# Half of the first layer's modulation tiles beside the latent projections, with two weight buffers; the last branch's sum on VectorE; the residual loaded into its accumulator

## The chip, the cores and the metric

One core of a Trainium2 chip runs the whole kernel. The metric is the device time of one execution in microseconds: the median of the kernel's runs is 2621.69 us, from 2621.12 to 2623.41 in three runs.

The engines go by their short names in the profile: PE is TensorE, PEld its weight load, DVE is VectorE, ACT is ScalarE, POOL is GpSimd, SP is the engine that issues all of this kernel's transfers.

## What is computed

The reference is a diffusion trunk of two layers (called 0 and 1 here, as in the code), over 512 latent and 128 context tokens of width 1024. Each layer is a mixer and an MLP:

```
mod  = silu(cond) @ w_mod + b_mod        # six vectors of 1024 per layer, for two conditionings
h    = rms_norm(x) * (1 + mod[1]) + mod[0]
cols = h @ w_in                          # GLA, MLA latents, differential attention, gates
y_a, y_b, y_c = gla(cols), mla(cols), diff_attention(cols)
m    = sum over b of sigmoid(h @ w_gate[b]) * (y_b @ w_o[b])
x    = x + mod[2] * (m @ w_out)
h    = rms_norm(x) * (1 + mod[4]) + mod[3]
x    = x + mod[5] * (relu(h @ w1)**2 @ w2)
```

The latent tokens are modulated by one conditioning, the context tokens by the other. So `mod` of both layers depends on the conditionings alone and may be computed at any time before its use: kinds 0 and 1 before a layer's first norm, kind 2 in the output projection, 3 and 4 in the second norm, 5 behind the MLP.

## The kernel before

**Layout.** Activations lie with features on the partitions and the 640 tokens along the free dimension, in halves of 256 and 384 columns (`HALVES`). Every operand of a matmul is a pair of a high and a low part, and each product is three matmuls (L104 to L106 in `mm3`): high by high, high by low, low by high.

**Weights.** `load_w` (L89) loads a block of 512 KB (256 KB for wo) on SP (L94), ScalarE casts the high part (L97), and VectorE subtracts for the low one (L99); while `pool_lo` is set, in the latent projections, POOL does that subtraction. The buffers are those of tag w (wraw 2, whi and wlo 3); while pool w2 is open, blocks alternate with a second set (xraw 1, xhi and xlo 3).

**Modulation.** `mod_tile` (L202) computes 128 of the 6 x 1024 outputs of one layer: a load of 512 KB (L206, tile modw, one buffer), and two multiply-and-sum operations on VectorE (L209, one for each conditioning; their throwaway output is mjunk, the sum goes to modv). After every fourth tile `mod_fin` (L233) adds the bias. The first 16 tiles of layer 0 come at the start of the kernel, twelve of them by TensorE (`mod_first`) and four in buffers of their own (tile sraw). The other 80 tiles, 32 of layer 0 (kinds 2 to 5) and 48 of layer 1, are handed out one by one by `mod_some` (L248), all of them behind the attention branches of layer 0: 8 + 4 + 4 in the three merges (`MERGE_MODS`), 8 in the output projection (`OUT_MODS`), 56 in the MLP, one after each block of w1 and w2. Layer 1 has none to do.

**The latent projections.** `mla_down` (L607) projects h to the query latent, the key-value latent and a small tail, token tile by token tile of 128, with three generators: two tiles of each are started, then each is drained. It stands at the beginning of a layer, behind the first norm. In layer 0 it runs from about 50 to 115 us.

**Merge.** `merge` (L1203) runs once per branch b. For each of eight blocks m of 128 features it projects the branch's output by wo (L94), multiplies by the gate into th (L1232, VectorE), sums into mg[m] (L1234, POOL; branches 1 and 2), and for branch 2 splits mg[m] into mh and ml (L137 on ScalarE, L138 on VectorE), the input of the output projection.

**Output projection.** `out_proj` (L1257) takes m by m: a block of wout, the residual as xin (L1270, one load for each half, three buffers), the matmuls, and the addition into the new accumulator xs[m] (L1247, `add_res`), then the sum of squares for the next norm (L267, sqacc). mg and xs share the eight buffers of tag x. The MLP (L1281) follows.

**Order.** The instructions of an engine are not issued in the order of the source: a planner arranges them at compile time by when their inputs are ready. The trace shows it: the first block of w1 is loaded ahead of the last blocks of wout. SP issues all loads in one queue, and one that waits for its buffer holds those behind it.

**Pools.** A pool's space is reused when it closes; `mj` holds modw, mjunk and condb (the conditioning spread over the partitions). Tiles of a pool opened over the space of another wait until that one's tiles were used for the last time.

Of the kernel before, what the change touches and what calls it, by code (L numbers as in the profile page):

```python
# [11 lines left out]
F32 = mybir.dt.float32  # L12
# [4 lines left out]
ALU = mybir.AluOpType  # L17
# [20 lines left out]

SCAN_PROJ = (1, 2)
GROUPS = ((0, 1), (2, 3, 4))  # L40
MERGE_MODS = ((1, 1, 1, 1, 1, 1, 1, 1), (0, 1, 0, 1, 0, 1, 0, 1), (1, 1, 1, 1, 0, 0, 0, 0))
OUT_MODS = (2, 2, 2, 2, 0, 0, 0, 0)
MERGE_AHEAD = 3

SKEW = (3, 6, 3)
# [1 line left out]
TAGS = {  # L47
    "wraw": ("w", 2), "whi": ("w", 3), "wlo": ("w", 3), "xraw": ("w2", 1), "xhi": ("w2", 3), "xlo": ("w2", 3), "hh": ("h", 8), "hl": ("h", 8),
    "sm_m": ("small", 4), "sm_b": ("small", 4), "sm_s0": ("small", 4), "sm_s1": ("small", 4), "sm_r": ("small", 4),
    "rowb": ("tab", 1), "tabmq": ("tab", 1), "tabmk": ("tab", 1), "lampr": ("tab", 1),  # L50
    "krn": ("tab", 1), "aan": ("tab", 1), "krg": ("tab", 1), "krc": ("tab", 1), "sskr": ("tab", 1),
    "nlam": ("tab", 1), "ghalf": ("tab", 1), "gsub": ("tab", 1), "gqk": ("tab", 1),
    "x": ("x", 8), "sqacc": ("nrm", 1), "sqt": ("nrm", 2), "nt": ("nrm", 3),
    "yb": ("yb", 2), "yc": ("dif", 4), "pd0": ("dif", 4), "pd1": ("dif", 2), "gth": ("gth", 3),
# [5 lines left out]
    "mla_sq": ("mla", 1), "mla_v": ("mla", 6), "mla_kn": ("mla", 9), "mla_qn": ("mla", 5),  # L60
    "mla_pp": ("mla", 2), "mla_qh": ("mla", 2), "mla_ql": ("mla", 2), "mla_kh": ("mla", 2), "mla_kl": ("mla", 2),
    "pt": ("att", 4), "mla_th": ("mla", 2), "mla_tl": ("mla", 2), "mla_tmp": ("mla", 1), "mla_tmp2": ("mla", 1),
    "rt1_32": ("tab", 1), "rt2_32": ("tab", 1), "rt1_64": ("dfr", 1), "rt2_64": ("dfr", 1),
# [5 lines left out]
    "xin": ("xin", 3), "mjunk": ("mj", 1), "condb": ("mj", 1), "modw": ("mj", 1), "mraw": ("st", 2), "sraw": ("st", 4), "maskf": ("st", 2), "mrow": ("st", 2), "uh": ("mlp", 8), "ul": ("mlp", 8), "relu": ("mlp", 3),  # L69
# [5 lines left out]
class Net:  # L75
# [531 lines left out]
    def mla_down(self, l, h):  # L607

        self.qdn = [self.S([128, 384], F32, "qdn") for t in range(5)]
        self.kvn = [self.S([128, 256], F32, "kvn") for t in range(5)]  # L610
        gens = [self.proj_tail(l, h), self.proj_nat(l, 2, h, self.kvn),
                self.proj_nat(l, 3, h, [q[:, 0:256] for q in self.qdn])]
        for g in gens:
            for _ in range(2):
                next(g)
        for g in gens:
            self.drain(g)

    def mla_latent(self, l):

# [582 lines left out]
    def merge(self, l, b, h):  # L1203

        nc = self.nc
        if b == 0:
            self.ys = {}
            self.drain(self.merge_in(0))
        ys = self.ys[b]
        nxt = self.merge_in(b + 1) if b < 2 else iter(())  # L1210
        outs = []
        if b == 0:
            self.mg = [self.S([128, T], F32, "x") for m in range(8)]
        mg = self.mg
        for m in range(8):
            t = mg[m] if b == 0 else self.S([128, T], F32, "th")
            if (b, m) in self.early:
                nc.sync.dma_start(t, self.gd[b][:, m])
            else:
                for p, (c0, c1) in zip(self.gates(l, b, m, h), HALVES):  # L1220
                    nc.scalar.activation(t[:, c0:c1], p[:, :c1 - c0], AF.Tanh, scale=0.5)
            wo = self.load_w(self.a["wo"][l, b, m], [128, 4, 128])
            ws = [(wo[0][:, k], wo[1][:, k]) for k in range(4)]
            if b == 2:
                mh = self.S([128, T], F32R, "mh")
                ml = self.S([128, T], F32R, "ml")
                outs.append((mh, ml))
            for i, (c0, c1) in enumerate(HALVES):
                n = c1 - c0
                p = self.P([128, 512], "g")  # L1230
                self.gemm(p[:, :n], ws, ys, c0, c1)
                nc.vector.scalar_tensor_tensor(t[:, c0:c1], t[:, c0:c1], 1.0, p[:, :n], op0=ALU.add, op1=ALU.mult)  # L1232
                if b:
                    nc.gpsimd.tensor_tensor(mg[m][:, c0:c1], mg[m][:, c0:c1], t[:, c0:c1], op=ALU.add)  # L1234
                if b == 2:
                    self.split(mg[m][:, c0:c1], n, mh[:, c0:c1], ml[:, c0:c1])
            if m >= MERGE_AHEAD:
                next(nxt, None)
            self.mod_some(MERGE_MODS[b][m])
        self.drain(nxt)  # L1240
        return outs

    def add_res(self, l, kind, m, half, p, src, dst, o=0):

        c0 = HALVES[half][0]
        for p0, p1, s in PARTS[half]:
            self.nc.vector.scalar_tensor_tensor(  # L1247
                dst[:, p0:p1], p[:, p0 - c0:p1 - c0], self.moda[l][:, kind * 8 + m, s:s + 1], src[:, p0 - o:p1 - o],
                op0=ALU.mult, op1=ALU.add)

    def order(self, head, tail):
# [5 lines left out]
    def out_proj(self, l, ms, xsrc):  # L1257
        self.stat_begin()
        xs = [self.S([128, T], F32, "x") for k in range(8)]
        wts = {}  # L1260
        self.norm_begin()
        for m, i in self.order(0, SKEW[0]):
            if (m, i) == (8 - SKEW[0], 1):
                self.norm(l, 1, xs, 0)
            if m not in wts:
                w = self.load_w(self.a["wout"][l, m], [128, 8, 128])
                wts[m] = [(w[0][:, k], w[1][:, k]) for k in range(8)]
            c0, c1 = HALVES[i]
            xin = self.S([128, 384], F32, "xin")
            self.nc.sync.dma_start(xin[:, :c1 - c0], xsrc(m)[:, c0:c1])  # L1270
            p = self.P([128, 512], "g")
            self.gemm(p[:, :c1 - c0], wts[m], ms, c0, c1)
            self.add_res(l, 2, m, i, p, xin, xs[m], c0)
            self.stat_add(xs[m], i)
            if i and l == 0:
                self.mod_some(OUT_MODS[m])
        self.norm(l, 1, xs, 1)
        return xs
# [65 lines left out]
    def run(self):  # L1344
        nc, tc, a = self.nc, self.tc, self.a
        self.pools, self.open, self.turn, self.pool_lo = {}, set(), 0, True
        with ExitStack() as top:
# [13 lines left out]
            nx.enter_context(self.pool("nrm", "st", "mj"))  # L1361
# [20 lines left out]
            for l in range(DEPTH):  # L1382
                for st in (nx, xp):
                    st.close()
                xp, nx, pm, w2 = self.layer(l, self.h, w2, pm)
            for st in (nx, xp, pm, w2):
                st.close()

    def layer(self, l, h, w2, ps):
        nc, tc, a = self.nc, self.tc, self.a  # L1390
        self.tables(l)
        self.ghalf = self.S([128, 1], F32, "ghalf")
        nc.vector.tensor_scalar(self.ghalf, self.vec[:, l, 16:17], 0.5, None, op0=ALU.mult)
# [7 lines left out]
        fl, lat, latT, mla = ExitStack(), ExitStack(), ExitStack(), ExitStack()  # L1401
        fl.enter_context(self.pool("gth"))
        latT.enter_context(self.pool("latT"))
        lat.enter_context(self.pool("lat"))
        self.fillq.append(self.gla_r(l, h, range(4)))
        self.fillq.append(self.gates_early(l, 0, h, range(8)))
        self.fillq.append(self.gates_early(l, 1, h, range(8)))
        self.fillq.append(self.gates_early(l, 2, h, range(8)))
        self.pool_lo = True
        self.mla_down(l, h)  # L1410
        self.pool_lo = False
        self.fill(4)
# [53 lines left out]

        pm = self.psum("pn")
        w2 = ExitStack()
        xp, mo, nrm, xin, mrg, mrb = (ExitStack() for _ in range(6))
        self.pending = [(l, i) for i in range(16, 48)] if l == 0 else []  # L1470
        if l + 1 < DEPTH:
            self.pending += [(l + 1, i) for i in range(48)]
        if self.pending:
# [11 lines left out]
        ms = self.merge(l, 2, h)  # L1485
        mrg.close()
        w2.enter_context(self.pool("w2", side="right"))
        xin.enter_context(self.pool("xin"))
        xs = self.out_proj(l, ms, (lambda m: a["x"][:, m]) if l == 0 else (lambda m: self.xs_dram[:, m]))
        xin.close()  # L1490
        mo.close()
        with self.pool("mlp"):
            self.mlp(l, xs, self.h, l + 1 == DEPTH)
# [147 lines left out]
```

## Time and profile before

| | |
|---|---|
| median of the runs | 2621.69 us (2621.12 to 2623.41) |
| the profiled execution | 2621.01 us, its span 2619.2 us |
| mean granted TensorE clock | 0.985 |
| DVE, ACT, POOL busy | 61%, 45%, 17% of the span |
| chain that ended last, by engine | PE 56%, DVE 7%, ACT 3% |
| the same by line, the first that is not PE's | DMA modw<-wmod 2% |
| tiles of modulation behind the attention branches | 80, their loads from 597.2 to 1267.2 us |

The profile is of one execution on the chip. Its span runs from the first instruction to the last; the profiled execution's own time is 1.8 us longer. A row of a windows view gives how long each engine was busy in a stretch; the times behind that are in the same order on every row. A row of a waits view says which operation stood, what came last of what it waited for, and the total, the number and the longest of these waits. A row of a timeline gives the start and the duration, and in brackets how long the engine stood before it and for what.

### The profile page before, as it was taken

What the parts mean: (1) busy time and instruction counts of PE and PEld (TensorE: products, weight loads), DVE (VectorE), ACT (ScalarE), POOL (GpSimd) and SP (SyncE); (2) the same over time, 40 slices, a digit from 0 to 9 for tenths busy, and PEclk for the clock granted to TensorE, in tenths of its full rate; (3) what the DMA queues carried; (4) which work ended last, traced back from release to release, by engine and by line L of the source; (5) the groups of instructions that cost most, each with busy time, mean ns of one, the idle gap of its engine ahead of it and who ended that gap; (6) DMA issues with size and microseconds to landing.
All of it is one profiled execution on the core that took longest, in us unless ns stands there. A gap on an engine that the chain in (4) does not pass through costs nothing.

```text
span 2619.2 us, 45102 instructions
## 1 busy us (share of the span) xinstructions
PE 2517.7 (96%) x17596; PEld 2433.6 (93%) x17596; DVE 1594.1 (61%) x3635; ACT 1189.1 (45%) x2323; POOL 446.5 (17%) x582
## 2 busy tenths in 40 slices
PE   6999999899998999999989999998999999999999
PEld 3988999898998999999989889998989999999999
DVE  7387666676676876666565776666764455333332
ACT  4477677556322332231334767775652334132230
POOL 2022242110041011020221222511001201010010
PEclk8999999999998999999999999999999999999999
DMA  6111112312655454444321111122225342222221
GB/s 256 41 47 69 50 57 69 93 63 74 228 183 182 138 161 153 153 146 145 121 79 41 56 62 65 41 70 94 80 94 190 104 131 88 74 73 76 78 73 49
DMA packets 109589, 265.03 MB, mean 101 GB/s; under 512 B 12288, under 2 KB 46336, under 8 KB 108608
## 3 DMA queue, kind: packets, MB, share of 16 engines
q1 hardware_dynamic: 109376, 262.15, 30.1%
q8 instruction: 139, 2.28, 0.4%
q14 instruction: 74, 0.61, 0.1%
HBM read 232.71 MB, written 29.39 MB: 100 GB/s over the span
## 4 chain that ended last, share of the span: by engine, by line
PE 56%; DVE 7%; ACT 3%; issue 2%; DMA 2%; POOL 1%; SPq 0%; DVEq 0%; POOLq 0%; ACTq 0%
PE g L104 15%; PE g L105 15%; PE g L106 15%; DMA modw<-wmod 2%; PE f L104 1%; PE go L504 1%; PE f L105 1%; PE f L106 1%; DVE mjunk L209 1%; PE y L1024 1%; DVE sm_m L752 1%; PE g L820 1%; DMA xraw<-wout 1%; DVE wlo L99 0%; PE g L1016 0%
## 5 line engine op out<-in xcount | busy, mean ns | idle before, releaser
L97 ACT CAST whi<-wraw 128x1024 fp32r<-128x1024 f32 (+2 forms) x236 | 220.0, 933 | 414.5 <-PE g L105 346.4
L99 DVE TENSOR_TENSOR wlo<-wraw,whi 128x1024 fp32r<-128x1024 f32 (+3 forms) x230 | 256.9, 1118 | 210.8 <-ACT whi L97 203.9
L104 PE MATMUL g<-hh,whi 128*128 128x256 f32 (+1 forms) x992 | 311.7, 314 | 5.8 <-DVE gla_t L603 4.2
L106 PE MATMUL g<-hh,wlo 128*128 128x256 f32 (+1 forms) x992 | 310.0, 313 | 2.1 <-DVE wlo L99 2.1
L105 PE MATMUL g<-hl,whi 128*128 128x256 f32 (+1 forms) x992 | 309.8, 312 | 0.0
L1298 POOL TENSOR_TENSOR relu<-relu 128x256 f32<-128x256 f32 (+1 forms) x128 | 113.4, 887 | 801.1 <-ACT uh L1297 798.9
L209 DVE CUSTOM_DVE_ANT_0 mjunk<-modw,condb 128x1024 bf16<-128x1024 f32 x160 | 197.8, 1236 | 60.7 <-DMA modw<-wmod 60.1
L97 ACT CAST xhi<-xraw 128x1024 fp32r<-128x1024 f32 (+1 forms) x80 | 83.7, 1046 | 280.7 <-PE g L105 258.0
L1247 DVE SCALAR_TENSOR_TENSOR x<-g,moda,x 128x256 f32<-128x256 f32 (+1 forms) x192 | 78.4, 435 | 198.7 <-PE g L106 198.7
L104 PEld LDWEIGHTS g<-hh,whi 128*128 128x128 f32 x992 | 189.3, 191 | 7.3 <-issue 4.6
L106 PEld LDWEIGHTS g<-hh,wlo 128*128 128x128 f32 x992 | 189.5, 191 | 2.3 <-DVE wlo L99 2.3
L105 PEld LDWEIGHTS g<-hl,whi 128*128 128x128 f32 x992 | 189.6, 191 | 0.0
L104 PE MATMUL g<-hh,xhi 128*128 128x384 f32 (+1 forms) x544 | 168.1, 309 | 0.0
L106 PE MATMUL g<-hh,xlo 128*128 128x384 f32 (+1 forms) x544 | 168.0, 309 | 0.0
L105 PE MATMUL g<-hl,xhi 128*128 128x384 f32 (+1 forms) x544 | 167.8, 308 | 0.0
L105 PE MATMUL g<-ul,whi 128*128 128x384 f32 (+1 forms) x512 | 158.0, 309 | 0.6 <-DVE ul L1299 0.6
L104 PE MATMUL g<-uh,xhi 128*128 128x384 f32 (+1 forms) x512 | 158.2, 309 | 0.0
L106 PE MATMUL g<-uh,xlo 128*128 128x384 f32 (+1 forms) x512 | 158.0, 309 | 0.0
L105 PE MATMUL g<-ul,xhi 128*128 128x384 f32 (+1 forms) x512 | 158.0, 309 | 0.0
L106 PE MATMUL g<-uh,wlo 128*128 128x384 f32 (+1 forms) x512 | 158.0, 309 | 0.0
L104 PE MATMUL g<-uh,whi 128*128 128x384 f32 (+1 forms) x512 | 157.9, 308 | 0.0
L1234 POOL TENSOR_TENSOR x<-x,th 128x256 f32<-128x256 f32 x64 | 78.3, 1230 | 464.4 <-DVE th L1232 452.6
(445 smaller groups left out, 7751.5 us busy)
## 6 DMA issues: line engine op xcount, KB each, us to landing
modw<-wmod SPq DMA_DIRECT2D x80, 512.0 KB, 3.5
wraw<-w SPq DMA_DIRECT2D x64, 512.0 KB, 3.6
xraw<-w SPq DMA_DIRECT2D x64, 512.0 KB, 3.5
wraw<-wfm SPq DMA_DIRECT2D x62, 512.0 KB, 3.5
wraw<-wn SPq DMA_DIRECT2D x36, 512.0 KB, 3.7
wraw<-wo SPq DMA_DIRECT2D x48, 256.0 KB, 3.1
yin<-yd SPq DMA_DIRECT2D x24, 320.0 KB, 3.6
gd<-gth SPq DMA_DIRECT2D x36, 192.0 KB, 1.9
```

The source lines that it names most:

```text
L97: nc.scalar.copy(hi, raw)
L99: eng.tensor_tensor(lo, raw, hi.bitcast(F32), op=ALU.subtract)
L104: mm(out, wh, xh, start=first, stop=False)
L105: mm(out, wh, xl, start=False, stop=False)
L106: mm(out, wl, xh, start=False, stop=last)
L209: nc.vector.tensor_tensor_reduce(out=junk, in0=w, in1=self.condb[:, s], scale=1.0, scalar=0.0, op0=ALU.mult, op1=ALU.add, accum_out=self.m ...
L504: nc.tensor.matmul(p[:, hd], km[:, hd, cs], qm[:, hd, cs])
L752: nc.vector.tensor_reduce(out=nm, in_=sc, axis=ax, op=ALU.max, negate=True)
L820: nc.tensor.transpose(p[:, i * 256 + j * 128:i * 256 + j * 128 + 128], pts[j][:, (k0 + i) * 128:(k0 + i) * 128 + 128], self.ident)
L1234: nc.gpsimd.tensor_tensor(mg[m][:, c0:c1], mg[m][:, c0:c1], t[:, c0:c1], op=ALU.add)
L1247: self.nc.vector.scalar_tensor_tensor(dst[:, p0:p1], p[:, p0 - c0:p1 - c0], self.moda[l][:, kind * 8 + m, s:s + 1], src[:, p0 - o:p1 - o], ...
L1298: nc.gpsimd.tensor_tensor(r[:, :n], r[:, :n], r[:, :n], op=ALU.mult)
```

## The change

- `EARLY_MODS` = 12: `pending` is filled before `mla_down`, and `mla_down` of layer 0 computes one modulation tile after each token tile of its generators (12 in all). `MERGE_MODS` and `OUT_MODS` hand out 4 + 4 + 0 and 4 tiles; the MLP's 56 stay.
- modw gets two buffers. Pool mj is opened on the other side of the memory at the start, and stays open until `mla_latent` is done.
- Pools gth and latT are opened before the tables of a layer are computed, and seven small tables (tabmq, tabmk, krn, krg, krc, rt1_32, rt2_32) move from pool tab to latT.
- In merge, the sum of branch 2 is VectorE's instead of POOL's, in both layers.
- In the output projection the residual is loaded by eight transfers of 320 KB straight into the accumulator tiles xs[m], and `add_res` adds in place; pool xin is gone.

```diff
-MERGE_MODS = ((1, 1, 1, 1, 1, 1, 1, 1), (0, 1, 0, 1, 0, 1, 0, 1), (1, 1, 1, 1, 0, 0, 0, 0))
-OUT_MODS = (2, 2, 2, 2, 0, 0, 0, 0)
+EARLY_MODS = 12
+MERGE_MODS = ((1, 0, 1, 0, 1, 0, 1, 0), (0, 1, 0, 1, 0, 1, 0, 1), (0, 0, 0, 0, 0, 0, 0, 0))
+OUT_MODS = (1, 1, 1, 1, 0, 0, 0, 0)
...
-    "mjunk": ("mj", 1), "condb": ("mj", 1), "modw": ("mj", 1)
+    "mjunk": ("mj", 1), "condb": ("mj", 1), "modw": ("mj", 2)
...
+    def mod_early(self, n):
+        while n > 0 and self.left > 0:
+            self.left -= 1
+            n -= 1
+            self.mod_some(1)
...
         for g in gens:
             for _ in range(2):
                 next(g)
+                self.mod_early(1)
         for g in gens:
-            self.drain(g)
+            for _ in g:
+                self.mod_early(1)
+        self.mod_early(EARLY_MODS)
...
                 if b:
-                    nc.gpsimd.tensor_tensor(mg[m][:, c0:c1], mg[m][:, c0:c1], t[:, c0:c1], op=ALU.add)
+                    (nc.vector if b == 2 else nc.gpsimd).tensor_tensor(mg[m][:, c0:c1], mg[m][:, c0:c1], t[:, c0:c1], op=ALU.add)
...
         xs = [self.S([128, T], F32, "x") for k in range(8)]
+        for m in range(8):
+            self.nc.sync.dma_start(xs[m], xsrc(m))
...
-            xin = self.S([128, 384], F32, "xin")
-            self.nc.sync.dma_start(xin[:, :c1 - c0], xsrc(m)[:, c0:c1])
             p = self.P([128, 512], "g")
             self.gemm(p[:, :c1 - c0], wts[m], ms, c0, c1)
-            self.add_res(l, 2, m, i, p, xin, xs[m], c0)
+            self.add_res(l, 2, m, i, p, xs[m], xs[m])
...
         self.pool_lo = True
+        self.pending = [(l, i) for i in range(16, 48)] if l == 0 else []
+        self.left = EARLY_MODS if l == 0 else 0
         self.mla_down(l, h)
         self.pool_lo = False
         self.fill(4)
         self.mla_latent(l)
         lat.close()
+        mj.close()
         w2.close()
```

## Rows read from the trace of the kernel before

**Rows 1.** The page, part 1: busy time of the engines

```profile
PE 2517.7 (96%) x17596; PEld 2433.6 (93%) x17596; DVE 1594.1 (61%) x3635; ACT 1189.1 (45%) x2323; POOL 446.5 (17%) x582
```

**Rows 2.** Windows: us, PE, PEld, DVE, ACT, POOL busy; PEclk; DMA share; GB/s

```profile
679.50:710.60 31.10, 29.25 (x195) 27.96 (x195) 25.03 (x47) 10.30 (x16) 0.00 (x0) 1.00 0.87 303
710.60:743.10 32.50, 29.13 (x195) 28.38 (x194) 28.78 (x47) 6.41 (x10) 17.94 (x14) 1.00 0.64 212
743.10:817.20 74.10, 72.03 (x483) 71.83 (x482) 50.88 (x86) 20.67 (x39) 23.10 (x17) 0.98 0.47 160
817.20:949.80 132.60, 121.64 (x789) 120.12 (x788) 104.70 (x214) 51.00 (x94) 18.19 (x17) 0.94 0.50 164
1979.00:2007.10 28.10, 28.10 (x194) 28.10 (x194) 14.85 (x27) 8.70 (x15) 0.00 (x0) 1.00 0.66 224
2007.10:2035.30 28.20, 28.20 (x195) 28.20 (x194) 15.31 (x28) 6.33 (x11) 16.29 (x15) 1.00 0.55 171
2035.30:2105.40 70.10, 70.10 (x481) 70.10 (x480) 31.22 (x44) 22.84 (x40) 15.33 (x16) 1.00 0.29 92
2105.40:2221.50 116.10, 115.68 (x790) 114.68 (x789) 68.36 (x147) 49.85 (x91) 14.14 (x17) 1.00 0.35 114
```

**Rows 3.** Windows of tile modw alone: us, DVE busy; PEclk; DMA; GB/s

```profile
679.50:743.10 63.60, 20.83 (x17) 1.00 0.75 256
743.10:817.20 74.10, 25.23 (x20) 0.98 0.47 160
817.20:949.80 132.60, 36.35 (x30) 0.94 0.50 164
```

**Rows 4.** Waits of PE, 679.5 to 949.8: total, times, longest

```profile
PE g L106 <- DVE wlo L99: 6.0, 5, 2.1
```

**Rows 5.** Timeline of all engines, 822 to 828: start, us, engine, operation

```profile
822.38 1.23 DVE L209 CUSTOM_DVE_ANT_0 mjunk<-modw,condb 128x1024 bf16<-128x1024 f32 x1 [3.62 <-DMA modw<-wmod]
...
824.67 0.41 DVE L1232 SCALAR_TENSOR_TENSOR th<-th,g 128x256 f32<-128x256 f32 x1
...
827.29 0.58 PE L104 MATMUL g<-mh,whi 128*128 128x256 f32 x1 [7.55 <-ACT mh L137]
```

**Rows 6.** Waits of DVE, 679.5 to 949.8

```profile
DVE mjunk L209 <- DMA modw<-wmod: 24.8, 16, 3.6
```

**Rows 7.** Tile modw: its loads, issue to landing

```profile
DMA to landing us min/median/max: 3.3/3.5/5.6
```

**Rows 8.** Windows of layer 0's start, columns as in group 2

```profile
65.60:101.10 35.50, 35.50 (x305) 35.50 (x304) 5.05 (x11) 13.44 (x40) 4.78 (x25) 1.00 0.07 21
33.00:65.60 32.60, 27.15 (x100) 14.81 (x100) 28.26 (x63) 17.02 (x36) 14.43 (x14) 0.77 0.60 212
```

**Rows 9.** Timelines of DVE and of POOL at the start

```profile
34.32 1.27 DVE L304 SCALAR_TENSOR_TENSOR hl<-nt,moda,hh 128x256 fp32r<-128x256 f32 x3
...
37.92 4.20 DVE L304 SCALAR_TENSOR_TENSOR hl<-nt,moda,hh 128x256 fp32r<-128x256 f32 x4 [0.22 <-ACT hh L303]
...
39.68 1.91 POOL L99 TENSOR_TENSOR xlo<-xraw,xhi 128x768 fp32r<-128x768 f32 x1 [0.30 <-ACT xhi L97]
...
59.72 2.38 POOL L99 TENSOR_TENSOR xlo<-xraw,xhi 128x1024 fp32r<-128x1024 f32 x1 [3.42 <-ACT xhi L97]
```

**Rows 10.** Lines by form, POOL 743:832, DVE 2035:2221: count | busy, mean ns

```profile
L1234 POOL TENSOR_TENSOR x<-x,th 128x384 f32<-128x384 f32 x10 | 18.5, 1849 | 21.3 <-DVE th L1232 14.4 <-DVE moda L237 6.8
...
L267 DVE TENSOR_TENSOR sqacc<-sqacc,sqt 128x384 f32<-128x384 f32 x7 | 3.9, 553 | 0.6 <-ACT sqt L266 0.6
```

**Rows 11.** Timelines of SP and of DVE at layer 1's seam

```profile
2104.65 0.42 SPq L94 DMA_DIRECT2D xraw<-wout  x1
2108.14 0.33 SPq L94 DMA_DIRECT2D wraw<-w  x1
...
2109.56 0.56 DVE L138 TENSOR_TENSOR ml<-x,mh 128x384 fp32r<-128x384 f32 x1 [1.45 <-ACT mh L137]
```

**Rows 12.** Lines by form, DVE, 20 to 32.5

```profile
L209 DVE CUSTOM_DVE_ANT_0 mjunk<-sraw,condb 128x1024 bf16<-128x1024 f32 x8 | 9.8, 1220 | 0.1
```

More of the change, by code (lines that the diff above doesn't have):

```diff
@@ L49 @@
     "sm_m": ("small", 4), "sm_b": ("small", 4), "sm_s0": ("small", 4), "sm_s1": ("small", 4), "sm_r": ("small", 4),
-    "rowb": ("tab", 1), "tabmq": ("tab", 1), "tabmk": ("tab", 1), "lampr": ("tab", 1),
-    "krn": ("tab", 1), "aan": ("tab", 1), "krg": ("tab", 1), "krc": ("tab", 1), "sskr": ("tab", 1),
+    "rowb": ("tab", 1), "tabmq": ("latT", 1), "tabmk": ("latT", 1), "lampr": ("tab", 1),
+    "krn": ("latT", 1), "aan": ("tab", 1), "krg": ("latT", 1), "krc": ("latT", 1), "sskr": ("tab", 1),
     "nlam": ("tab", 1), "ghalf": ("tab", 1), "gsub": ("tab", 1), "gqk": ("tab", 1),
@@ L62 @@
     "pt": ("att", 4), "mla_th": ("mla", 2), "mla_tl": ("mla", 2), "mla_tmp": ("mla", 1), "mla_tmp2": ("mla", 1),
-    "rt1_32": ("tab", 1), "rt2_32": ("tab", 1), "rt1_64": ("dfr", 1), "rt2_64": ("dfr", 1),
+    "rt1_32": ("latT", 1), "rt2_32": ("latT", 1), "rt1_64": ("dfr", 1), "rt2_64": ("dfr", 1),
     "tabdq": ("dfr", 1), "tabdk": ("dfr", 1), "df_q": ("dfr", 5), "df_k": ("dfr", 5), "df_v0": ("dfr", 5), "df_v1": ("dif", 5),
@@ L68 @@
     "yin": ("mrg", 2), "yh": ("mrg", 4), "oyh": ("mrb", 4), "oyl": ("mrb", 4), "yl": ("mrg", 4), "th": ("mrg", 2), "mh": ("mo", 8), "ml": ("mo", 8),
-    "xin": ("xin", 3), "mjunk": ("mj", 1), "condb": ("mj", 1), "modw": ("mj", 1), "mraw": ("st", 2), "sraw": ("st", 4), "maskf": ("st", 2), "mrow": ("st", 2), "uh": ("mlp", 8), "ul": ("mlp", 8), "relu": ("mlp", 3),
+    "mjunk": ("mj", 1), "condb": ("mj", 1), "modw": ("mj", 2), "mraw": ("st", 2), "sraw": ("st", 4), "maskf": ("st", 2), "mrow": ("st", 2), "uh": ("mlp", 8), "ul": ("mlp", 8), "relu": ("mlp", 3),
 }
@@ L1241, in merge, with add_res @@
         return outs
-    def add_res(self, l, kind, m, half, p, src, dst, o=0):
+    def add_res(self, l, kind, m, half, p, src, dst):
         c0 = HALVES[half][0]
@@ L1247, in add_res @@
             self.nc.vector.scalar_tensor_tensor(
-                dst[:, p0:p1], p[:, p0 - c0:p1 - c0], self.moda[l][:, kind * 8 + m, s:s + 1], src[:, p0 - o:p1 - o],
+                dst[:, p0:p1], p[:, p0 - c0:p1 - c0], self.moda[l][:, kind * 8 + m, s:s + 1], src[:, p0:p1],
                 op0=ALU.mult, op1=ALU.add)
@@ L1360, in run @@
             xp.enter_context(self.pool("x"))
-            nx.enter_context(self.pool("nrm", "st", "mj"))
+            mj = ExitStack()
+            mj.enter_context(self.pool("mj", side="right"))
+            nx.enter_context(self.pool("nrm", "st"))
             pm = self.psum("pn")
@@ L1384, in run, with layer @@
                     st.close()
-                xp, nx, pm, w2 = self.layer(l, self.h, w2, pm)
+                xp, nx, pm, w2 = self.layer(l, self.h, w2, pm, mj)
             for st in (nx, xp, pm, w2):
                 st.close()
-    def layer(self, l, h, w2, ps):
+    def layer(self, l, h, w2, ps, mj):
         nc, tc, a = self.nc, self.tc, self.a
+        fl, lat, latT, mla = ExitStack(), ExitStack(), ExitStack(), ExitStack()
+        fl.enter_context(self.pool("gth"))
+        latT.enter_context(self.pool("latT"))
         self.tables(l)
@@ L1400, in layer @@
         self.mid, self.fillq, self.early, self.up, self.raw, self.rqd = False, [], set(), {}, {}, {}
-        fl, lat, latT, mla = ExitStack(), ExitStack(), ExitStack(), ExitStack()
-        fl.enter_context(self.pool("gth"))
-        latT.enter_context(self.pool("latT"))
         lat.enter_context(self.pool("lat"))
@@ L1468, in layer @@
         w2 = ExitStack()
-        xp, mo, nrm, xin, mrg, mrb = (ExitStack() for _ in range(6))
-        self.pending = [(l, i) for i in range(16, 48)] if l == 0 else []
+        xp, mo, nrm, mrg, mrb = (ExitStack() for _ in range(5))
         if l + 1 < DEPTH:
@@ L1487, in layer @@
         w2.enter_context(self.pool("w2", side="right"))
-        xin.enter_context(self.pool("xin"))
         xs = self.out_proj(l, ms, (lambda m: a["x"][:, m]) if l == 0 else (lambda m: self.xs_dram[:, m]))
-        xin.close()
         mo.close()
```

## The prediction

> **What bounds the kernel now.** The page comes first: TensorE is busy for 96% of the span, VectorE for 61% [rows 1]. So TensorE bounds it, and the change can win only time in which TensorE stands or runs at a lower clock. Where that is, a comparison inside this one trace tells. Both layers issue the same matmuls in the three merges and in the output projection with the MLP's first tiles (up to the first matmul of w2), but only in layer 0 do modulation tiles run there. In layer 0 the four stretches take 31.1, 32.5, 74.1 and 132.6 us, in layer 1 28.1, 28.2, 70.1 and 116.1, there with TensorE busy nearly throughout at full clock [rows 2]. The excess is 3.0 + 4.3 + 4.0 + 16.5 = **27.8 us**, and I take it as the ceiling: with no modulation left there, layer 0 would run like layer 1.
>
> What makes the excess? VectorE is busy for 25.0, 28.8, 50.9 and 104.7 us there, against 14.9, 15.3, 31.2 and 68.4 [rows 2]; the difference, 79.7 us, is about what the modulation's operations take, 82.4 us [rows 3]. TensorE meets it at second hand: 6.0 us in five waits for wlo [rows 4], and 7.55 us once, at 827.29, for mh, at the seam from merge 2 to the output projection. Read the chain back from there: ScalarE's mh waits for POOL's sum, that for the gate product th, at 824.67 on VectorE, and th came behind a mjunk that had itself stood 3.62 us for its load [rows 5]. The fourth stretch has a granted clock of 0.94, so for a part of it the lower level, 1.2 GHz. Of its 16.5 us, (132.6 - 121.6) - (116.1 - 115.7) = 10.6 us are more idle time, and 121.6 - 115.7 = 5.9 us the slower matmuls [rows 2].
>
> **Part 1: twelve tiles move.** Of the 24 tiles that the source hands to layer 0's merges and output projection 12 stay (4 + 4 + 0 + 4) and 12 go beside mla_down. In the four stretches ran 17 + 20 + 30 mjunk operations, two per tile, so 33.5 tiles, the MLP's first among them [rows 3]; some 21.5 should be left.
>
> Merges 0 and 1: 8 tiles after, where 8.5 ran before, so the work hardly shrinks. VectorE was busy for 53.8 us of 63.6; less half a tile, 1.2, that is 52.6 us in the 56.3 that layer 1 needs [rows 2]. It just fits. What goes is the backlog behind them and the waiting for one buffer (part 2). Bounds for what stays of 7.3 us: nothing, or all. I leave 4, near the middle, because 3.7 us of slack is little. Gain 3.3.
>
> Merge 2: it gets none of its own. VectorE falls from 50.9 us towards the 31.2 of layer 1, where TensorE never stood [rows 2]. Gain 4.0; bounds 0 and 4.
>
> Output projection: 8 tiles become 4, and no backlog comes in. The 7.55 us need a mjunk ahead of th at the seam [rows 5]; with none handed out in merge 2 it should go, and the slow matmuls with it. Bounds for what stays of 16.5: nothing, or half, as half of the tiles stay. I take 3, nearer to nothing, since the longest wait loses its cause. Gain 13.5.
>
> **Part 2: two modw buffers.** VectorE stood 24.8 us in 16 waits for modw here [rows 6]. With one buffer a load goes out only when the second mjunk has read the tile before, and lands 3.5 us later [rows 7], while two mjunk are 2 x 1.23 us [rows 5]. With two buffers a tile costs about (3.5 + 2.5 + 0.3) / 2 = 3.2 us, an estimate with 0.3 for issuing. TensorE feels this only through wlo, th and mh, so its worth is inside the gains above.
>
> **Part 3: the new place.** Twelve tiles are 24 x 1.23 = 29.5 us of VectorE. From 65.6 to 101.1 us TensorE is full with the latent projections, VectorE busy for 5.05 of 35.5 us, the DMA share 0.07 [rows 8]: 30.4 us are free. At 3.2 us a tile they need 38 us, from about 62 to 100. The cover is that free time; without it the price is 29.5 us. Queued behind a mjunk there are VectorE's copies of the latent accumulators out of PSUM, late by one or two mjunk, 2.5 us, with six g banks to carry TensorE meanwhile: 0.
>
> The two loads that find free buffers can go out early, among the first latent weights. From 33 to 65.6 us TensorE is idle for 5.5 us at a granted clock of 0.77, and the DMA share is 0.60 [rows 8]. Two loads ahead of a wanted one on SP delay it by 2 x 3.5 = 7 us; behind it by nothing. I take 2, below the middle, since in the source they come after the first weights. Cost 2, bounds 0 and 7.
>
> VectorE is slow there beside POOL's lo splits: four hl take 4.20 us from 37.92, with a split of 1.91 us on POOL at 39.68, where three took 1.27 at 34.32 [rows 9]. The Trainium skill (SBUF — State Buffer, Who interferes with whom) says that a VectorE instruction with two SBUF inputs and a GpSimd instruction that reads SBUF exclude each other for a whole instruction; the trace agrees, 4.20 us against 1.7 for four at the free rate. By that rule the move costs something, mjunk having two SBUF inputs: an estimate from it and the split of 2.38 us is 4 x 2.38 = 9.5 us for two early tiles, and the sum would be 2612. By the rows alone the last split ends at 59.72 + 2.38 = 62.1 [rows 9] and the tiles run behind it: 0, bounds 0 and the 7 us above.
>
> The tables' pool: krn, krg, krc and the rope tables come to lie where the norm's buffers were, so their POOL steps wait for the norm's end. Their first user is behind the latent projections: 0; bound 2.4, by POOL's longest operation there [rows 9].
>
> **Part 4: merge 2's sums on VectorE.** POOL's sum of 384 columns took 1849 ns, a VectorE addition of that shape (sqacc) 553 [rows 10]. Sixteen sums, half of them shorter, add at most 16 x 0.55 = 8.8 us to VectorE in each layer, with 38.9 us free in merge 2 of layer 1 [rows 2]: 0. At the seam mh comes 1.3 us earlier, a gain only where TensorE waits for it; layer 0's wait is counted above. Bounds -1.3 and +1 per layer.
>
> **Part 5: the residual into its accumulator.** Sixteen xin loads go, eight loads of xs[m] come, into the buffers that mg had: each must wait until mh and ml of that m are split off. The bytes are the same: 0. The place in SP's queue is the risk (rival B).
>
> **Sum.** 3.3 + 4.0 + 13.5 - 2 = 18.8 us. The profiled execution took 2621.0 us (span 2619.2, 1.8 around it), 0.7 below the median of 2621.7. 2621.0 - 18.8 = 2602.2: I say **2602**, own range 2593 (all of the excess, no cost) to 2611 (rival A's bounds).
>
> **Rivals.** A: VectorE still bounds the early merges and half of the output projection. The 7.3 us stay, 8.2 of 16.5 stay: gain 4.0 + 8.3 - 2 = 10.3, so 2611. For it: 52.6 us of work in 56.3. Against: the second buffer and the missing backlog. Chance 0.14.
>
> B: the xs loads stand on SP ahead of wout's. The last waits for ml of mg[7], in layer 1 at 2109.56 + 0.56, while the first xraw of wout went out at 2104.65 [rows 11]: late by 5.5 us, TensorE stands and loses clock, by layer 0's seam (10.6 idle, 5.9 clock) some 6 to 9 us in each layer. 2602 + 13 = 2615, between 2614 and 2620. Against: SP's order follows what can go, as the load of the MLP's first weight at 2108.14, ahead of wout loads that came later, shows [rows 11]. Chance 0.10.
>
> C, slower: VectorE takes the early tiles ahead of layer 0's first norm, as it took eight mjunk of 1.22 us between the norm's steps before 32.5 us [rows 12]. All 24 operations on the path cost 29.5 us against 18.8 + 2 = 20.8: 2630. It decides from 17 operations (17 x 1.23 = 20.9). Against: the source puts the first projection tile before them. Chance 0.05.
>
> D: the planner leaves the tiles where they were, since VectorE and SP take what is ready by its rank: 2621. Chance 0.04.
>
> **Numbers.** Main case 0.67, A 0.14, B 0.10, C 0.05, D 0.04. A measurement of this kernel can tell about 0.2%, 5.2 us, from no change. Faster by more: main, A and half of B, 0.86. The same: the rest of B and D, less a little, 0.08. Slower: C and some of what I don't see, 0.06. The range, 2593 to 2615, holds the main case, A and half of B.
>
> **What would show it.** Right: 24 more mjunk between about 60 and 105 us with TensorE full; the first three stretches near 30, 30 and 70 us; the 7.55 us wait for mh gone, the fourth stretch's clock at 0.97 or more. Wrong: as many waits for wlo in merges 0 and 1 (A), TensorE standing for a wout weight in layer 1 too (B), the latent projections starting late (C), as many mjunk in merge 2 as now (D).

## The result: slower, and the profile after

The changed kernel takes 2638.81 us (2638.53 to 2639.01 in four runs), the kernel before 2621.6: a ratio of 1.0064, 95% interval 1.0051 to 1.0077. It was forecast at 2602 and is 17 us slower. The profiled execution took 2638.66 us, its span 2636.8.

The page and the chain of the changed kernel (lines of its source stand 1 to 11 further down than before):

```profile
PE 2519.8 (96%) x17596; PEld 2436.6 (92%) x17596; DVE 1595.3 (61%) x3667; ACT 1188.4 (45%) x2323; POOL 406.6 (15%) x550
...
PE 73%; DVE 13%; ACT 5%; DMA 5%; issue 3%; POOL 1%; SPq 0%; DVEq 0%; ACTq 0%; POOLq 0%
```

No engine is busy for more than 3 us longer than in [rows 1]; time was lost in waits. Where, the same matmuls tell: every run issues 17,596 of them, so the start of the n-th bounds the same stretch in each trace. Outside three stretches the traces differ by 3 us at most (4 to 6 in e7 and e8). "Start" runs from the first norm's matmul at 33.1 us to the one at 115.2 in the trace before, "four" are the four stretches of [rows 2], "MLP" is what follows them to 1262. "mjunk" counts the tile operations in the four; one that crosses a bound between two windows may be counted in both, one or two in a row of the table. The stretches are those of the one profiled execution, the ratio is of medians; the profiled executions of e4, e6, e7 and e9 took 3 to 4.5 us more than their medians, the others at most 1.4.

| run | start | four stretches | MLP | mjunk in the four | ratio to before |
|---|---|---|---|---|---|
| before | 82.1 | 270.3 | 312.4 | 67 | |
| after | 94.7 | 272.1 | 314.2 | 97 | 1.0064 |
| e1 rest alone | 81.3 | 265.6 | 312.6 | 67 | 0.9974 |
| e2 no early tiles, two buffers | 81.0 | 274.8 | 313.6 | 102 | 1.0015 |
| e3 rope tables early | 87.3 | 272.1 | 314.3 | 97 | 1.0036 |
| e4 MLP tiles held | 95.0 | 254.9 | 324.6 | 49 | 1.0017 |
| e5 as e1, POOL's sum | 81.5 | 269.4 | 313.2 | 64 | 0.9998 |
| e6 one buffer | 103.5 | 271.9 | 311.8 | 63 | 1.0069 |
| e7 one buffer, tables early, drain only | 99.2 | 274.7 | 311.9 | 63 | 1.0078 |
| e8 as e7, held | 100.1 | 249.7 | 312.1 | 40 | 0.9999 |
| e9 one buffer from the merges on | 94.9 | 272.2 | 311.7 | 63 | 1.0032 |
| e10 tables early, held, one buffer later | 87.0 | 249.6 | 311.8 | 39 | 0.9936 |
| e11 as e10, eight early tiles | 83.6 | 249.6 | 311.6 | 47 | 0.9917 |
| e12 as e1, held | 81.3 | 264.7 | 312.3 | 63 | 0.9966 |

So the start lost 12.6 us, the four stretches gained nothing (1.8 more), the MLP lost 1.8. Up to merge 0 the changed kernel is 13.8 us behind (693.3 us against 679.5); the 13.9 of two expectations below is that shift, not the start alone.

**The four stretches.** Windows of the changed kernel, all engines (columns of [rows 2]), then tile modw alone:

```profile
693.30:724.40 31.10, 28.80 (x195) 28.07 (x194) 27.01 (x50) 10.29 (x16) 0.00 (x0) 1.00 0.89 300
724.40:752.60 28.20, 28.20 (x195) 28.20 (x194) 27.55 (x44) 6.44 (x10) 17.25 (x12) 1.00 0.71 228
752.60:829.50 76.90, 71.70 (x483) 70.57 (x482) 67.55 (x123) 20.33 (x38) 7.09 (x5) 1.00 0.66 220
829.50:965.40 135.90, 120.01 (x788) 118.05 (x788) 127.74 (x259) 51.63 (x94) 14.94 (x15) 0.95 0.55 179
```

```profile
693.30:724.40 31.10, 11.85 (x10) 1.00 0.89 300
724.40:752.60 28.20, 11.75 (x9) 1.00 0.71 228
752.60:829.50 76.90, 37.88 (x30) 1.00 0.66 220
829.50:965.40 135.90, 59.23 (x48) 0.95 0.55 179
```

Against [rows 3] there are 97 tile operations, not 67, although twelve tiles had been moved away. Merge 2, to which the source now hands no tile, has 30. The fourth stretch holds the beginning of the MLP too, where MLP tiles have their place. Windows of tile modw that end at the last matmul of the output projection leave those out; the kernel before, then the changed one:

```profile
679.50:817.10 137.60, 46.06 (x37) 0.99 0.60 204
817.10:891.00 73.90, 23.15 (x19) 0.88 0.60 202
```

```profile
693.30:829.30 136.00, 61.48 (x48) 1.00 0.72 240
829.30:901.50 72.20, 36.55 (x30) 0.91 0.66 215
```

To that point the source of the kernel before hands out 48 operations (24 tiles), and 56 ran; the changed one hands out 24, and 78 ran. What came too early is the MLP's: held back by a dependence, it is gone (e4, e8). The planner puts these tiles ahead of their place, and the room that the move made was filled. VectorE is busy for 127.7 of 135.9 us in the last stretch, where [rows 2] has 104.7 of 132.6. The wait at the seam is still there. Timeline of the changed kernel, all engines, against [rows 5]:

```profile
837.23 1.23 DVE L210 CUSTOM_DVE_ANT_0 mjunk<-modw,condb 128x1024 bf16<-128x1024 f32 x1 [0.60 <-DMA modw<-wmod]
...
838.38 0.42 DVE L1245 TENSOR_TENSOR x<-x,th 128x256 f32<-128x256 f32 x1
...
838.83 0.40 ACT L138 CAST mh<-x 128x256 fp32r<-128x256 f32 x1 [2.87 <-DVE x L1245]
...
839.29 0.90 PE L105 MATMUL g<-mh,whi 128*128 128x256 f32 x2 [7.29 <-ACT mh L138]
```

The sum is VectorE's now, 0.42 us long, and it stands behind a mjunk itself; TensorE waits 7.29 us for mh where it was 7.55.

**The start.** Waits of PE in the latent projections of the changed kernel, 67.1 to 113.8 us; the kernel before has none there [rows 8]:

```profile
PE g L105 <- DVE aan L381: 4.8, 1, 4.8
PE g L106 <- POOL xlo L100: 2.9, 1, 2.9
```

The window of that stretch, beside the first row of [rows 8]:

```profile
67.10:113.80 46.70, 38.96 (x305) 38.59 (x304) 30.67 (x60) 13.45 (x40) 19.09 (x42) 0.93 0.38 127
```

It is 46.7 us long instead of 35.5; 7.7 us are these two waits, the remaining 3.5 the matmuls at a lower clock after them (38.96 us busy instead of 35.50). The later wait first had an earlier cause. POOL, SP and DVE in the timelines of the changed kernel:

```profile
65.72 0.64 POOL L341 TENSOR_TENSOR tabmq<-rope,rowb 128x128 f32<-128x128 f32 x1
66.33 4.87 POOL L349 TENSOR_TENSOR tabmq<-rope,rowb 128x16 f32<-128x16 f32 x8
...
72.56 1.47 POOL L349 TENSOR_TENSOR tabmk<-rope,rowb 128x16 f32<-128x16 f32 x8
74.00 2.33 POOL L100 TENSOR_TENSOR xlo<-xraw,xhi 128x1024 fp32r<-128x1024 f32 x1
```

```profile
66.17 0.42 SPq L681 DMA_DIRECT2D krc<-krc  x1
76.35 0.33 SPq L95 DMA_DIRECT2D xraw<-wfm  x1
76.77 23.46 SPq L207 DMA_DIRECT2D modw<-wmod  x8
```

```profile
81.16 1.22 DVE L210 CUSTOM_DVE_ANT_0 mjunk<-modw,condb 128x1024 bf16<-128x1024 f32 x1 [8.14 <-DMA modw<-wmod]
...
102.12 1.22 DVE L210 CUSTOM_DVE_ANT_0 mjunk<-modw,condb 128x1024 bf16<-128x1024 f32 x1
...
103.37 0.18 DVE L381 COPY aan<-g 128x32 f32<-128x32 f32 x1
```

The rope tables, which now wait for the norm's space, run on POOL from 65.7 and hold up the split of a latent weight to 74.0 (first wait). That split frees xraw, for which SP's queue stands from 66.6 to 76.35; behind it stand the modw loads. So VectorE stands 8.14 us, its next mjunk begins at 81.16, and fourteen of them lie in VectorE's order ahead of the copy that empties a PSUM bank. It comes at 103.37 (second wait). In the kernel before, that token tile's copy came at 79.24.

The stretch ahead of that one, from 33.1 to 65.6 us in the kernel before, took 33.9 us instead of 32.5. There two early tiles run between the norm's steps. Timeline of VectorE in the kernel before, then those of VectorE, ScalarE and TensorE in the changed one:

```profile
52.50 1.30 DVE L237 TENSOR_TENSOR moda<-modv,bmod 128x8 f32<-128x8 f32 x1
```

```profile
52.06 1.23 DVE L210 CUSTOM_DVE_ANT_0 mjunk<-modw,condb 128x1024 bf16<-128x1024 f32 x1
...
53.21 2.29 DVE L238 TENSOR_TENSOR moda<-modv,bmod 128x8 f32<-128x8 f32 x1
...
55.53 1.31 ACT L311 ACTIVATE hh<-nt,moda 128x256 fp32r<-128x256 f32 x3 [2.58 <-DVE moda L238]
...
56.09 0.53 PE L105 MATMUL g<-xhi,hh 128*128 128x192 f32 x1 [4.76 <-ACT hh L311]
```

The modulation that hh needs (moda) stands behind four mjunk and is ready at 55.50 instead of 53.80. TensorE starts on that hh at 56.09, where it was 54.40 (1.6 us later, counted from the start of the stretch).

### The profile page after: what moved, and what is told of

Read it like the earlier page. It is cut to its first block, busy times and chain, and to the rows that moved or that the text cites. A ratio compares the mean times of both kernels' runs of the same rounds, so it can differ in the third digit from the quotient of the medians.

```text
span 2636.8 us, 44977 instructions
## 1 busy us (share of the span) xinstructions
PE 2519.8 (96%) x17596; PEld 2436.6 (92%) x17596; DVE 1595.3 (61%) x3667; ACT 1188.4 (45%) x2323; POOL 406.6 (15%) x550
## 4 chain that ended last, share of the span: by engine, by line
PE 73%; DVE 13%; ACT 5%; DMA 5%; issue 3%; POOL 1%; SPq 0%; DVEq 0%; ACTq 0%; POOLq 0%
PE g L105 17%; PE g L106 17%; PE g L107 17%; PE f L105 3%; DMA modw<-wmod 2%; PE f L106 2%; PE go L512 2%; PE f L107 2%; DVE mjunk L210 2%; PE y L1035 1%; DVE wlo L100 1%; DVE sm_m L763 1%; PE g L831 1%; DVE hl L312 1%; PE gt L107 1%
## 5 line engine op out<-in xcount | busy, mean ns | idle before, releaser
L100 DVE TENSOR_TENSOR wlo<-wraw,whi 128x1024 fp32r<-128x1024 f32 (+3 forms) x230 | 249.3, 1084 | 222.8 <-ACT whi L98 216.8
L1309 POOL TENSOR_TENSOR relu<-relu 128x256 f32<-128x256 f32 (+1 forms) x128 | 105.0, 822 | 964.9 <-ACT uh L1308 943.0
L1258 DVE SCALAR_TENSOR_TENSOR x<-g,moda,x 128x256 f32<-128x256 f32 (+1 forms) x240 | 98.1, 435 | 245.6 <-PE g L107 245.6
L98 ACT CAST xhi<-xraw 128x1024 fp32r<-128x1024 f32 (+1 forms) x80 | 83.6, 1045 | 281.2 <-PE g L106 260.0
L105 PE MATMUL f<-hh,whi 128*128 128x256 f32 (+1 forms) x448 | 141.1, 315 | 4.6 <-ACT gth L1196 4.4
```

The source lines that it names most:

```text
L98: nc.scalar.copy(hi, raw)
L100: eng.tensor_tensor(lo, raw, hi.bitcast(F32), op=ALU.subtract)
L105: mm(out, wh, xh, start=first, stop=False)
L1258: self.nc.vector.scalar_tensor_tensor(dst[:, p0:p1], p[:, p0 - c0:p1 - c0], self.moda[l][:, kind * 8 + m, s:s + 1], src[:, p0:p1], op0=ALU ...
L1309: nc.gpsimd.tensor_tensor(r[:, :n], r[:, :n], r[:, :n], op=ALU.mult)
```

## The experiments

The theories at first: P, the second buffer draws the MLP's tiles forward and the start loses to early tiles and tables; R, merge 2's sums or the residual's loads eat the gain. The first four runs test them.

**e1, the rest alone.** One buffer, no early tiles, the old hand-out:

```diff
-EARLY_MODS = 12
+EARLY_MODS = 0
-MERGE_MODS = ((1, 0, 1, 0, 1, 0, 1, 0), (0, 1, 0, 1, 0, 1, 0, 1), (0, 0, 0, 0, 0, 0, 0, 0))
-OUT_MODS = (1, 1, 1, 1, 0, 0, 0, 0)
+MERGE_MODS = ((1, 1, 1, 1, 1, 1, 1, 1), (0, 1, 0, 1, 0, 1, 0, 1), (1, 1, 1, 1, 0, 0, 0, 0))
+OUT_MODS = (2, 2, 2, 2, 0, 0, 0, 0)
...
-    ... "modw": ("mj", 2) ...
+    ... "modw": ("mj", 1) ...
```

> The changed kernel with one modw buffer, no early tiles and the old hand-out (8 + 4 + 4 and 8 tiles): what is left of the change is VectorE's sum, the residual's loads and the tables' new pool. Theory P (the second buffer lets tiles of the MLP run ahead into the merges, and the start loses its time to the early tiles and to the tables' POOL work ahead of a weight split): layer 0's merges and output projection as in the kernel before, within 2 us; at the start only the tables' part, 0 to 5 us; 2621 to 2627. Rival R (the sums or the residual's loads cost 15 to 20 us there and eat the gain): those stretches 15 us longer than before, 2635 or more.

Measured: 2615.2 against 2622.18, ratio 0.9974 (0.9965 to 0.9984). R falls: the rest is a gain. P's range, 2621 to 2627, is missed too: the four stretches fell by 4.7 us where P had them within 2 us of before. The tables' move costs nothing at the start here, 81.3 us against 82.1: in e1 POOL makes the last split at 60.74 and the tables only after it, at 65.72. Without early tiles nothing is late for them to delay.

**e2, no early tiles, but two buffers** (e1's diff without the lines on modw).

> The changed kernel without early tiles and with the old hand-out, but two modw buffers. Theory P: MLP tiles run ahead, some 40 tiles in layer 0's four stretches against 33.5 before, so these stretches are 0 to 8 us longer than before, and the start loses only the tables' part: 2622 to 2634. Rival R: as the first run, 2635 or more. If two buffers are a gain by themselves: below 2619.

Measured: 2626.0, ratio 1.0015 (1.0006 to 1.0024). Against e1 the second buffer alone costs 0.4%: 102 tile operations, 51 tiles, in the four stretches, more than the 40 expected, and 274.8 us.

**e3, layer 0's rope tables early.** In a pool of their own, free from the start:

```diff
+RP = ("tabmq", "tabmk")
...
+            self.rp.enter_context(self.pool("rp", side="right"))
+            for n in RP:
+                TAGS[n] = ("rp", 1)
             w2.enter_context(self.pool("w2", side="right"))
```

> The changed kernel, with layer 0's two rope tables in space that is free from the start, so that POOL computes them before the latent weights are split. Theory P1 (the tables held up a weight split, that split held SP's queue, the modw loads came late and the latent accumulators' copies waited behind them): both waits of the start, 2.9 and 4.8 us with the slow matmuls behind them, shrink; start 2 to 6 us longer than before instead of 13.9, time 2627 to 2631. Theory P2 (the two waits are independent, the second is VectorE's own queue of 14 mjunk ahead of a copy): only the first goes, 4.6 us; 2633 to 2635. If the tables have no part: 2638 to 2640.

Measured: 2631.8, ratio 1.0036 (1.0021 to 1.005); the start takes 87.3 us, 5.2 above before. P1 holds, at the edge of its range (2631): with POOL free the split comes at 66.94 instead of 74.00, the modw loads go out from 72.67 instead of 76.77, the wait for xlo is gone, and the wait for the copy, which has mjunk ahead of it as before, shrinks from 4.8 to 2.1:

```profile
PE g L106 <- DVE aan L382: 2.1, 1, 2.1
```

**e4, the MLP's tiles held back.** A data dependence behind layer 0's output projection, which changes no value:

```diff
+    def hold(self, t):
+        c = self.condb[:, 0, 0:1]
+        self.nc.vector.scalar_tensor_tensor(c, t[:, 0:1], 0.0, c, op0=ALU.mult, op1=ALU.add)
...
         self.norm(l, 1, xs, 1)
+        if l == 0:
+            self.hold(xs[7])
         return xs
```

> The changed kernel, with one small VectorE operation behind the output projection of layer 0 that writes one column of condb from the last residual tile (times 0, plus itself): the MLP's tiles can't run before it. Theory P: only the 12 tiles handed out run in the merges and the output projection, these stretches come near to layer 1's (at most 8 us above), the start still loses 13.9: 2611 to 2620. Rival R: nothing gained there, 2636 to 2642.

Measured: 2626.54, ratio 1.0017 (1.0007 to 1.0026). The stretches fell by 15.4 us to 254.9, 12.4 above layer 1's 242.5, where P allowed 8; the time, 2611 to 2620, is missed, since the MLP took 324.6 us. It has 88 tile operations, no more than in the kernel before (89 between the same bounds), but with two buffers they crowd in behind the hold: the last mjunk starts at 1114.3 us instead of 1272.8. The MLP's matmuls wait for ul on VectorE (waits of PE, 947.5 to 1272):

```profile
PE g L106 <- DVE ul L1316: 8.2, 3, 5.1
```

**e5, e1 with POOL's sum in merge 2.**

```diff
-                    (nc.vector if b == 2 else nc.gpsimd).tensor_tensor(mg[m][:, c0:c1], mg[m][:, c0:c1], t[:, c0:c1], op=ALU.add)
+                    nc.gpsimd.tensor_tensor(mg[m][:, c0:c1], mg[m][:, c0:c1], t[:, c0:c1], op=ALU.add)
```

> The first run's kernel (one buffer, no early tiles, the old hand-out) with merge 2's sums back on POOL: of the rest only the residual's loads into the accumulators and the tables' pool are left. If VectorE's sums carry that run's gain of 0.26% (th no longer waits behind POOL at the seam): 2619 to 2623. If the residual's loads carry it (sixteen loads fewer on SP, one for both halves): 2613 to 2617. Merge 2 and output projection of layer 0 together: 206.7 us in the first case, 202 in the second.

Measured: 2622.28 against 2622.4, ratio 0.9998 (0.9988 to 1.0007). The gain of e1 is VectorE's sum; loads and pools together are worth nothing that can be measured. The two stretches took 73.8 + 131.2 = 205.0 us (202.0 in e1), between the two values expected.

**e6, the changed kernel with one buffer.**

```diff
-    ... "modw": ("mj", 2) ...
+    ... "modw": ("mj", 1) ...
```

> The changed kernel with one modw buffer and nothing else undone. The order of VectorE's instructions then has 50 operations of tiles between the first merge and the end of layer 0's output projection, where the kernel before has 54 and the changed one 74. Theory P (the second buffer draws MLP tiles forward): those stretches and the MLP fall by some 10 us against the changed kernel, to what the first run showed (265.6 us for the four stretches) or below, and the start still loses 5 to 13 us to tables and early tiles: 2617 to 2629. Rival (the early tiles alone are to blame and the buffers are free): the four stretches as in the changed kernel, 272 us; 2634 to 2640.

Measured: 2641.81, ratio 1.0069 (1.0052 to 1.0086): missed. The start takes 103.5 us. With one buffer VectorE stands for each tile's load, and the copies stand behind it (waits of PE and of DVE, 67.4 to 120):

```profile
PE g L105 <- DVE aan L381: 11.3, 3, 6.3
```

```profile
DVE mjunk L210 <- DMA modw<-wmod: 26.2, 8, 4.6
```

The early tiles need the second buffer. And the four stretches stay at 271.9 with 63 operations instead of 97: with one buffer, too, the planner fills up the room (52 operations to the end of the output projection, 24 handed out). The stretches are the rival's; the time lies a little above its range too.

**e7 and e8: one buffer, early tables, early tiles only in the drain;** e8 with the hold of e4 besides.

```diff
                 next(g)
-                self.mod_early(1)
```

> One modw buffer, layer 0's two rope tables in space free from the start, and the early tiles only behind the token tiles of the drain, not of the head (so no modw load goes ahead of the first latent weights). If the start's loss is the tables and the loads of the head: the start within 3 us of the kernel before, 2611 to 2618, no better than the first run by more than 4 us because tiles of the MLP fill the room. If it is VectorE's queue of mjunk ahead of the accumulators' copies, at any place in the latent projections: the start 4 to 10 us longer, 2618 to 2626.

> The seventh run's kernel with the small VectorE operation of the fourth, which holds the MLP's tiles back to the end of layer 0's output projection. Theory P: the four stretches come to 255 us as in the fourth run (270.3 before), and with one buffer the MLP is not crowded, 0 to 4 us above before where the fourth run had 12; with a start within 3 us: 2602 to 2612. If the held tiles crowd the MLP in any case: 2613 to 2622.

Measured: 2643.34, ratio 1.0078 (1.0062 to 1.0094), and 2623.36, ratio 0.9999 (0.999 to 1.0009). Both times are outside every range expected, by the start, which is 17 to 18 us longer than before: with one buffer it didn't help to leave out the head's tiles and to make the tables early. In e7 VectorE stands 2.2 to 3.7 us for each tile's load from 71 to 115 us, and the copies stand behind it. But e8 parts the two halves of the change cleanly: the four stretches fall by 20.6 us and the MLP stays at 312.1, so holding the tiles and pacing them by one buffer gives what the prediction had counted on.

**e9, two buffers early, one from the merges on.**

```diff
+        TAGS["modw"] = ("mj", 1)
         if self.pending:
             w2.enter_context(self.pool("mj", side="right"))
```

> The changed kernel, with two modw buffers for the early tiles as there, but one buffer for the tiles from the merges on; nothing else undone. Theory P' (with what the runs so far showed: the early tiles need the second buffer, the merges lose by it): the start as in the changed kernel, 13 us above before; in the four stretches some 25 fewer tile operations by the order than in the changed kernel, so 264 to 270 us instead of 272: 2630 to 2636. Rival (the second buffer is neutral in the merges, the sixth run's time there was 271.9 with one): 2637 to 2640.

Measured: 2630.34, ratio 1.0032 (1.002 to 1.0043). By the total it is P', by the stretches it is the rival: 272.2 us, as with two buffers, at 63 operations instead of 97. The gain against the changed kernel lies elsewhere, 2.5 us of it in the MLP. So between 63 and 97 the number of tile operations alone doesn't set the stretches' time; with 40 (e8) it is 249.7.

**e10 and e11: all three mendings** (e3, e4, e9), e11 with eight early tiles, four more handed to merge 2:

```diff
-EARLY_MODS = 12
+EARLY_MODS = 8
-MERGE_MODS = ((1, 0, 1, 0, 1, 0, 1, 0), (0, 1, 0, 1, 0, 1, 0, 1), (0, 0, 0, 0, 0, 0, 0, 0))
+MERGE_MODS = ((1, 0, 1, 0, 1, 0, 1, 0), (0, 1, 0, 1, 0, 1, 0, 1), (1, 0, 1, 0, 1, 0, 1, 0))
```

> The changed kernel with three mendings: layer 0's rope tables in space free from the start (as the third run), one modw buffer from the merges on, and the operation that holds the MLP's tiles back (as the fourth). Theory P': start 5 us above before (third run), the four stretches 250 (eighth run, 249.7), the MLP as before: 2602 to 2609, faster than every kernel so far. Rival (the MLP or the attention part takes it back): 2612 to 2620.

> The tenth run's kernel with 8 early tiles instead of 12; the four others are handed out in merge 2. If the start's 5 us come from the number of mjunk queued ahead of the accumulators' copies: 1 to 4 us less at the start, 0 to 4 us more in merge 2, 2600 to 2610. If they come from the first loads: the start unchanged, and 0 to 4 us slower than the tenth run.

Measured: 2604.78, ratio 0.9936 (0.9921 to 0.9951), and 2599.59, ratio 0.9917 (0.9902 to 0.9932). e11 beats both kernels. Its start is 3.4 us shorter than e10's, all of it in the latent projections (35.5 us against 38.8), while the stretch of the first loads is unchanged (34.0 against 34.1): so that gain came from the number of mjunk ahead of a copy, not from the first loads. With twelve tiles one wait for a copy is left (waits of PE in the latent projections of e10), with eight none:

```profile
PE g L106 <- DVE aan L386: 3.1, 1, 3.1
```

The windows of e11's four stretches, to be held against [rows 2]:

```profile
679.90:710.60 30.70, 29.18 (x194) 27.89 (x194) 24.98 (x46) 10.23 (x16) 0.00 (x0) 1.00 0.89 307
710.60:740.70 30.10, 28.79 (x196) 28.36 (x194) 26.74 (x43) 6.47 (x11) 16.70 (x13) 1.00 0.66 199
740.70:813.10 72.40, 71.06 (x483) 70.34 (x482) 54.62 (x100) 22.77 (x43) 4.77 (x4) 1.00 0.60 199
813.10:929.40 116.30, 115.30 (x788) 114.55 (x788) 86.00 (x179) 49.72 (x90) 14.97 (x15) 1.00 0.40 129
```

The last, 116.3 us, is layer 1's 116.1 at the full clock; merges 0 and 1 keep 4.5 us of their 7.3. At e11's seam no mjunk stands on VectorE (timeline of all engines):

```profile
811.72 0.41 DVE L1248 SCALAR_TENSOR_TENSOR th<-th,g 128x256 f32<-128x256 f32 x1
...
812.17 0.42 DVE L1250 TENSOR_TENSOR x<-x,th 128x256 f32<-128x256 f32 x1
...
812.63 0.41 ACT L139 CAST mh<-x 128x256 fp32r<-128x256 f32 x1 [1.70 <-DVE x L1250]
```

**e12, the hold without early tiles** (e1 with e4's lines).

> The first run's kernel (one buffer, no early tiles) with the operation that holds the MLP's tiles back. The four stretches keep 24 tiles instead of 33: if what counts is the number of tiles there, about a third of the excess goes, 257 to 262 us against 265.6 in the first run, 2607 to 2613; then early tiles are worth 3 to 8 us more beside it. If the number doesn't count, only their place: 2614 to 2617, as the first run.

Measured: 2613.7 against 2621.4, ratio 0.9966 (0.9954 to 0.9978); the four stretches 264.7, as e1. The stretches are those expected if the number doesn't count. Holding alone brings nothing clear: with all 24 tiles handed out there, mjunk still stand at the seam, and TensorE waits 3.5 us for mh. Early tiles empty the room, the hold keeps it empty; in the four stretches each alone is worth little (272 us in e9, 264.7 here, 265.6 in e1).

## Why the prediction was wrong

**Where the excess is: right.** The ceiling of 27.8 us stood: e11 takes 20.8 of it, the very sum forecast for the four stretches (3.3 + 4.0 + 13.5). That the sums agree is partly luck: merge 2 gave less than forecast (1.7), the output projection more (16.3), merges 0 and 1 2.8, and e11 has a hold, one buffer there and four tiles in merge 2, none of which the prediction had.

**Part 1 failed at "some 21.5 should be left".** 48.5 tiles ran in the stretches, and the forecast gain of 20.8 us there became a loss of 1.8. The hand-out in the source doesn't fix a tile's place: with one buffer 31.5 tiles still ran there (e9), with a dependence besides some 20 (e8). Of the surplus that the prediction saw, 33.5 tiles where the source hands out 24, most was the MLP's first ones in their own place, as it said (11 of the 19 operations, behind the output projection's last matmul); the other 8 had come ahead of theirs. That was the sign, a small one, that room would be refilled. "No backlog comes in" and "the longest wait loses its cause" were drawn from the same mistake. With the hold and one buffer, e8 shows the stretches as forecast (249.7 us; 270.3 - 20.8 = 249.5), with two buffers e4 does not (254.9).

Of the signs that the prediction named, the seam's wait stayed (7.29 us), the fourth stretch's clock was 0.95, and merge 2 had as many mjunk as before and ten more, which is D's sign.

**Part 2** was sized at nothing of its own. It costs 0.4% without early tiles (e2 against e1); with them, from the merges on, 8.5 us by the medians of after and e9 and 5.3 by their profiled spans; for the early tiles it is needed: without it the start takes 103.5 us instead of 94.7 (e6).

**Part 3 failed at "late by one or two mjunk, 2.5 us".** In VectorE's order fourteen mjunk lay ahead of the copy, not one or two; with their loads late, that was 4.8 us of wait and a lower clock. The 2 us for two loads ahead of the first weights came out near by luck: that stretch is 1.4 us longer than before (2.2 longer than e1's 31.7), but by VectorE, where two tiles stood ahead of the norm's moda, and not by SP's order, which was what was priced. The tables' pool, at 0 with a bound of 2.4, was the term that set it off: with the tables early 7.4 us of the 12.6 go (e3), while without early tiles the move costs nothing (e1). Four early tiles less take another 3.4 us off (e11 against e10). The two edits meet in SP's queue, and neither was priced with the other in place. Six g banks didn't carry TensorE.

The prediction looked for a price on VectorE beside POOL. The slower side here was POOL: eight small table operations took 4.87 us beside mjunk and 1.74 in e1, where VectorE ended the norm and then had short copies; in the changed kernel itself the next eight, from 72.56, after the last of those mjunk, took 1.47. The Trainium skill (SBUF — State Buffer, Who interferes with whom) says that issue order decides who blocks; these numbers don't contradict it, and no run here varies the order alone. By the estimate that the prediction drew from that section of the Trainium skill the sum would have been 2612, still faster.

**Part 4** was put at 0 with a gain of 1.3 as bound; it measured 0.24%, 6.3 us (e1 against e5, 0.9974 and 0.9998, each to about 0.1%). **Part 5** at 0: right, and rival B fell: layer 1's seam has no wait of TensorE in the changed kernel.

**The rivals.** Rival A's time was wrong; its picture, VectorE bounding the output projection, came true by more tiles there than A reckoned with. Rival C had the sign and the mechanism, early tiles ahead of what TensorE needs. Four of the 24 operations did stand in the norm's way, in a stretch that grew by 1.4 us; the larger part of the loss came at another place, ahead of the copies. D came closest in the four stretches, and had no loss at the start.

What stays open: which of merge 2's or the output projection's own tiles hold up the seam. Against layer 1's time e11 (16 and 15 operations there) loses nothing in the fourth stretch, e12 (21 and 25) 8 us, and no run lies between. Open too is why 63 operations in e9 cost as much there as 97 in the changed kernel.

## What to carry to other kernels

Moving work out of a stretch helped here only when nothing could move in: where a planner fills gaps, look at what stood ahead of its place before, and give later work a dependence that holds it. Filler on VectorE beside a full TensorE must not stand, in VectorE's order, ahead of what empties TensorE's accumulators; count the fillers in that order, not the free microseconds. Two edits that are free one at a time can meet in one queue, so price a space that comes free later with the other edit's delays in it.

## What the runs showed of the hardware

POOL's eight table operations of 16 columns took 1.74 us in e1 and 4.87 in the changed kernel beside mjunk: 2.8 times, for operations that share no data. With the waits of 4.8 and 2.9 us the granted clock of the latent projections was 0.93 over 46.7 us, and the slower matmuls cost 3.5 us more, nearly half of the waits themselves. The length of a wait alone doesn't tell the price: in e3 TensorE waited 2.1 us and the clock was 0.66 from 97 to 102 us, just behind it; in e10 it waited 3.1 us and the clock was 1.00 over all 38.8 us of the latent projections.
